# A quarter of the retention's value projection at the turn from feed-forward to mixing, and residual rows in spent W_out tiles

## The chip, the cores and the metric

The kernel runs on one core of a Trainium2 chip. The metric is the device time of one execution in microseconds (us): the median of several runs. The engines are TensorE (PE: matmuls; PEld: its weight loads), VectorE (DVE), ScalarE (ACT), GpSimd (POOL) and SyncE (SP), which here only issues DMAs. DMAs issued from POOL stand in POOL's queue, those from SP in SP's. Each engine works through its own instructions in order.

## What is computed

One layer of a bidirectional encoder trunk for 1024 tokens of width 1024, all in float32: a feed-forward layer, token mixing (retention and neighbourhood attention), and a second feed-forward layer, each between two RMS norms.

```python
def reference(x, ...):
    h = _swiglu(_rms_norm(x, ffn1_pre_norm), ffn1_w_in, ffn1_w_out)      # 1024 -> 2 x 2816 -> 1024
    x = x + 0.5 * _rms_norm(h, ffn1_post_norm)
    m = _token_mixing(_rms_norm(x, mix_pre_norm), w_mix_in, ...)
    x = x + _rms_norm(m, mix_post_norm)
    h = _swiglu(_rms_norm(x, ffn2_pre_norm), ffn2_w_in, ffn2_w_out)
    return x + 0.5 * _rms_norm(h, ffn2_post_norm)

def _token_mixing(u, w_in, ...):
    rq, rk, rv, rg, nq, nk, nv, g_ret, g_na = jnp.split(u @ w_in, points, axis=-1)
    y = _bidirectional_retention(rotary(rq), rotary(rk), rv)              # rv: 1024 tokens x 1024
    y_ret = (silu(rg) * headnorm(y)) @ w_ret_out
    y_na = _neighborhood_attention(nq, nk, nv, rel_bias) @ w_na_out       # nv: 1024 tokens x 512
    return (sigmoid(g_ret) * y_ret + sigmoid(g_na) * y_na) @ w_out
```

The change touches the end of the first feed-forward layer, the projection `rv`, and the order in which that projection is computed.

## The kernel before

**Matmuls.** Every float32 operand is split into a high part (a rounding cast on ACT, line 61) and a low part (a subtraction on DVE, line 62). A product then takes three matmuls into one PSUM bank (`mm3`, lines 88 to 90): high by high, high by low, low by high. One call of `mm3` on 128 x 512 outputs is called a unit here. Weights come by `load_w`: one DMA of 512 KB from SP into a `wraw` buffer (line 72, four buffers), then two halves (`piece`), each split into a `wh` and a `wl` buffer (eight of each). PSUM has six banks tagged `ps` and two tagged `pt`.

**The first feed-forward layer** works with a 2 x 2 block scheme (Winograd's): seven products per block. Its second half, `ffn_out`, runs 77 steps: seven products (`a11, s1, s2, s3, a22, a12, s4`) of 11 steps each. W_out is held as four blocks of three tiles each (`tiles`; `tiles[1][0]` is the block b21, last read by the product a12). Product s4, steps 66 to 76, is the last one. As its four banks finish, the function `p3` completes the token tiles 4 to 7 (512 to 1023): squares, the scale from the norm (line 98, on POOL), the residual sum (line 659, on DVE), the store of the new row to x1 (line 660, on SP), and the next layer's norm (line 670, on DVE). The residual row of a token tile, 128 x 1024 values, is fetched by `xload`, for tiles 4, 5 and 6 at steps 68, 69 and 70, and for tile 7 after the end of tile 6. Tiles 0 to 3 take spent W_out tiles for it; tiles 4 to 7 take `wraw` buffers.

**The turn.** The normalized tiles 4 to 7 then have to be transposed on PE (`flip`, line 127) and combined into the operands of the next Winograd scheme (`put`, lines 282 to 294: a22, s3, s1, s2, s4, each split into high and low). The eight tiles of s1 to s4 share eight places with the W_out blocks b21 and b22 and two result tiles. PE gets other work between the flips from `first()`: the neighbourhood value projection nv of tokens 0 to 511 (`vproj(wnv, ...)`, 32 units, whose first two weight tiles are loaded ahead at steps 65 and 66), then the leading products of the first three jobs of the mixing projections (`mx.leads()`, 24 units). `Filler` hands out units: `FLIP_FILL` says how many stand before each of the four flips (8 each) and how many between a flip and the last split of its tile (2). What is left runs at once after the last flip.

**Mixing projections.** The 14 jobs of `mx.run` compute nq, nk, rq, rk, rg and two gates; the tokens 512 to 1023 of nv follow after the fourth job.

**Attention and retention.** `na_cores` (neighbourhood attention) and then `ret_cores` (retention) have many short matmuls with chains over DVE and ACT between them. A second filler, `products()`, supplies units between them: the retention's values rv in two halves of columns, each over the token groups (0,1,2), (3,4,5), (6,7), then the remaining gates, then the output projection of the attention. In a group of `vproj` each weight tile serves two steps of k for each token tile of the group. `NA_FILL` gives 12 units at first and 2 + 2 per iteration (34 iterations); `RET_FILL` gives 14 at first and, for each of the four heads, 2, then 2 in each of 7 backward steps, 4, 2, and 3 + 0 + 1 in each of the 8 forward steps.

**Order.** The program is written in one order; a scheduler at build time gives each instruction the priority of its place in the text, gives out buffers as they come free, and fixes the order of each engine's queue. On the chip that order is kept.

Of the kernel before, what the change touches and what calls it, by code (L numbers as in the profile page):

```python
# [10 lines left out]
F32 = mybir.dt.float32  # L11
# [7 lines left out]
P = 128  # L19
# [8 lines left out]
NHP = 4  # L28

NA_FILL = (12, 2, 2)  # L30
RET_FILL = (14, 2, 2, 4, 2, 3, 0, 1, 2)
FLIP_FILL = (8, 8, 8, 8, 2)
LOADS = (6, 9, 12, 15, 18, 22, 28, 33, 38)
NA_UNITS = ((0, 0, 0), (3, 1, 0), (1, 0, 1), (1, 0, 2), (4, 1, 1), (4, 1, 2), (2, 0, 3), (5, 1, 3))
KEY_OFF = (0, 8, 24, 32)
# [638 lines left out]
def ffn_out(c, tiles, q, blocks, w_out, gl, ep, tail, side={}):  # L674
# [3 lines left out]
    nc = c.nc  # L678
# [3 lines left out]
    later, rest, flips, xs = [], [], [], {}  # L682
# [8 lines left out]

    def xload(t):

        if t < 4 or ep.pre is None:
            tile = (tiles[0][1] + tiles[0][0])[t // 2]
            xs[t] = tile[:, t % 2 * 2:t % 2 * 2 + 2].rearrange("p k f -> p (k f)")
            nc.sync.dma_start(xs[t], ep.resid(t))
        else:
            xs[t] = c.raw(ep.resid(t))


    order = []
# [31 lines left out]
    def p7(u, b):  # L734
        tt(q[3][:, u], b, q[1][:, u], ALU.add)

        def more():
            xload(u)
            add(q[1][:, u], q[1][:, u], q[2][:, u], ALU.add)
            add(q[2][:, u], q[3][:, u], q[2][:, u], ALU.add)  # L740
            ep.square(u, 1, q[2][:, u], spare[u])
        later.extend((more, None))
# [17 lines left out]
    def p3(u, b):  # L760
        e = tt(q[1][:, u], b, q[1][:, u], ALU.add)
        out = q[1][:, u] if ep.pre is not None else q[3][:, u]
        ep.square(4 + u, 1, q[1][:, u], b if ep.pre is not None else spare[2 + u % 2], out, nc.vector if u == 3 else nc.gpsimd)
        g = ep.steps(4 + u, xs[4 + u], (q[0][:, u], out))
        next(g)
        rest.append(g)
        if u > 0:
            with c.tc.issue_after(e.ins):
                next(rest[u - 1])
        if u == 3:  # L770
            next(g)
        if ep.pre is not None:
            flips.extend(next(rest[j]) for j in ((), (), (0,), (1, 2, 3))[u])
        if u == 2 and 7 not in xs:
            xload(7)
# [32 lines left out]
    for n, (i, k) in enumerate(steps):  # L808
# [11 lines left out]
        if later and i > 3:  # L820
            f = later.pop(0)
# [377 lines left out]
def trunk_layer(ctx: ExitStack, tc, x, xt, g1a, w1i, w1o, g1b, gma, wmt, wnv, wrv, logits, dtab, rope, bias,  # L1199
                wro, wno, wmo, gmb, g2a, w2i, w2o, g2b, out):  # L1200
    nc = tc.nc
# [5 lines left out]
    c = Core(tc, const, wpool, psum, dram)  # L1207
# [3 lines left out]
    def dt(name, shape):  # L1211
        return dram.tile(shape, F32, name=name)
# [3 lines left out]
    d = {  # L1216
        "a21": dt("a21", [P, 4, 512]),
        "nq": dt("nq", [NHP, P, S]), "nk": dt("nk", [NHP, P, S]), "nv": dt("nv", [16, 64, 512]), "nvg": dt("nvg", [4, 4, P, 512]),
        "no": dt("no", [NHP, P, S]), "rq": dt("rq", [RH, P, S]), "rk": dt("rk", [RH, P, S]),
        "rv": dt("rv", [TT, P, D]), "rg": dt("rg", [8, P, S]), "ry": dt("ry", [8, P, S]),  # L1220
        "sr": dt("sr", [8, P, S]), "sn": dt("sn", [8, P, S]), "z": dt("z", [8, P, S]), "m": dt("m", [8, P, S]),
    }
# [6 lines left out]
    def pool(stack, name, side="left"):  # L1229
        return stack.enter_context(tc.tile_pool(name=name, bufs=1, side=side, reuse_waits="tile"))  # L1230
# [30 lines left out]
    ep = pool(ep_stack, "ep1")  # L1261
# [4 lines left out]
    ahead = {}  # L1266
# [9 lines left out]
    def xh(t, k):  # L1276

        return a21 if (t, k) == (1, 0) else wx.op(("a11", "a12", None, "a22")[2 * t + k])

    def vproj(src, groups, done):  # L1280

        for toks in groups:
            banks = {t: c.bank() for t in toks}
            for k in range(KT):
                if k % 2 == 0:
                    w = ahead.pop(k // 2) if k // 2 in ahead else c.load_w(src[k // 2])
                for t in toks:
                    tt = slice((t % 4) * P, (t % 4 + 1) * P)
                    c.mm3(banks[t], [q[:, k % 4, tt] for q in xh(t // 4, k // 4)], w[k % 2], k == 0, k == KT - 1)
                    yield  # L1290
            for t in toks:
                done(t, banks[t])

    evpool = []

    def ev():
        return evpool[0].tile([P, S], F32, tag="ev", name="ev", bufs=3)

    def done_nv(t, b):
        e = evpool[0].tile([P, 512], F32, tag="ev", name="ev", bufs=6 if len(evpool) == 1 else 4)  # L1300
        nc.scalar.copy(e, b)
        c.store(d["nv"][2 * t:2 * t + 2].rearrange("r c d -> (r c) d"), e)

    def done_rv(j):
        def f(t, b):
            e = ev()
            nc.scalar.copy(e[:, :512], b)
            c.store(d["rv"][t][:, j * 512:(j + 1) * 512], e[:, :512])
        return f


# [5 lines left out]
    mx = Pairs(c, wx, [(wmt[j[0]], wmt[j[1]]) for j in jobs], 3)  # L1317

    def first():
        yield from vproj(wnv, ((0, 1, 2, 3),), done_nv)  # L1320
        yield from mx.leads()

    fill = Filler(first())
    evpool[:] = [wx.tmp, None]
    for f, k in zip(rest, FLIP_FILL):
        fill(k)
        f = f()
        if f is not None:
            fill(FLIP_FILL[4])
            f()  # L1330
    g_stack.close()
    ep_stack.close()
    with tc.tile_pool(name="pa", bufs=1, reuse_waits="tile") as pa:
# [12 lines left out]
        for i, (_, _, f, g, fn) in enumerate(jobs):  # L1346
# [6 lines left out]
            def done(j):  # L1353
                h = j % 2
                dst = (f, g)[j // 2][:, h * 512:(h + 1) * 512]
                while swaps:
                    swaps.pop()()
                if fn == "rotary":
                    swaps.append(rotate(c, half(), parts[j], *tabs[h], dst))
                    return  # L1360
                if fn is not None:
                    nc.scalar.activation(parts[j], parts[j], fn)
                c.store(dst, parts[j])
# [7 lines left out]
            if i == NHP - 1:  # L1371
                for _ in vproj(wnv, ((4, 5, 6, 7),), done_nv):
                    pass
                for cb in range(4):
                    nc.sync.dma_start(d["nvg"][cb].rearrange("t (r c) d -> (t r) c d", r=4),
                                      d["nv"][:, KEY_OFF[cb]:KEY_OFF[cb] + 32, :])
# [2 lines left out]
    m_stack, o_stack = ExitStack(), ExitStack()  # L1379
    mix = pool(m_stack, "mix")  # L1380
    mix.tile([P, 40], F32, name="pad")
    evpool[:] = [mix]

    def gate(i, dst, halves=(0, 1)):

        w = c.load_w(wmt[i])
        e = ev()
        for h in halves:
            hs = slice(h * 512, (h + 1) * 512)
            b = c.bank()  # L1390
            for k in range(KT):
                ks = slice((k % 4) * P, (k % 4 + 1) * P)
                c.mm3(b, [p[:, ks] for p in w[k // 4]], [q[:, k % 4] for q in xh(h, k // 4)], k == 0, k == KT - 1)
                yield
            nc.scalar.activation(e[:, hs], b, AF.Sigmoid)
        hs = slice(halves[0] * 512, halves[-1] * 512 + 512)
        c.store(dst[:, hs], e[:, hs])

    def products():
        for j in range(2):  # L1400
            yield from vproj(wrv[j], ((0, 1, 2), (3, 4, 5), (6, 7)), done_rv(j))
        yield "rv"
        for i in range(4, 8):
            yield from gate(32 + i, d["sn"][i])
        for i in range(4):
            yield from gate(24 + i, d["sr"][i])
        for i in range(4, 8):
            yield from gate(24 + i, d["sr"][i], (1,))
        x1_stack.close()
        opool = pool(o_stack, "o", "right")  # L1410
        oop = [opool.tile([P, 4, S], F32R, name=f"o{q}") for q in "hl"]
        for i in range(4, 8):
            raw = c.raw(d["no"][i - 4])
            c.split(oop[0][:, i - 4], oop[1][:, i - 4], raw)
            yield from gate(24 + i, d["sr"][i], (0,))

        for i in range(8):
            if i % 2 == 0:
                w = c.load_w(wno[i // 2])
            e = ev()  # L1420
            nc.sync.dma_start(e, d["sn"][i])
            for h in range(2):
                hs = slice(h * 512, (h + 1) * 512)
                b = c.bank()
                for k in range(4):
                    c.mm3(b, [p[:, k * P:(k + 1) * P] for p in w[i % 2]], [q[:, k, hs] for q in oop], k == 0, k == 3)
                    yield
                nc.vector.tensor_tensor(e[:, hs], b, e[:, hs], ALU.mult)
            c.store(d["z"][i], e)
# [7 lines left out]
    with tc.tile_pool(name="ret", bufs=1, reuse_waits="tile") as ret:  # L1437
        ret_cores(c, ret, mix, d, dec, fill, RET_FILL)
    y_stack = ExitStack()
# [13 lines left out]
    for i0 in (0, 3, 6):  # L1453
        tiles = range(i0, min(i0 + 3, 8))
        m, z, w, banks = {}, {}, {}, {}
# [71 lines left out]
    w = [w2.tile([P, 4, 512], F32, name=f"w{i}") for i in range(12)]  # L1527
    tiles = [[[w[n] for n in m] for m in q] for q in (((11, 10, 9), (8, 7, 6)), ((2, 1, 0), (5, 4, 3)))]
# [84 lines left out]
```

## Time and profile before

| what | us |
|---|---|
| median of 3 runs | 2270.53 |
| lowest and highest run | 2268.02, 2271.82 |
| profiled execution, its own time | 2266.95 |
| span of the profiled execution, from first to last instruction | 2265.2 |

The profile lists busy time by engine, and windows of it by stretch of the span. Times in rows of the trace are microseconds from the start of the span; mean durations marked ns are nanoseconds. In a timeline a row has the start, the duration, the engine, the line of the kernel, the operation, and the tiles (out <- in); in brackets stands the idle time of that engine before it and what ended it. A row of PE lasts longer than the distance to the next one, since matmuls overlap; the pace is the distance from start to start. "Granted clock" is the share of PE's full clock that the chip granted. In the span, the first feed-forward layer ends at about 673 us, the turn follows, the mixing projections end at about 1003, attention at about 1190, and retention at about 1432.

### The profile page before, as it was taken

Reading aid. Unit: us, or ns where it says so; the run is one execution under the profiler, and the core shown is the slowest. Engines: PE = TensorE matmul, PEld = TensorE weight load, DVE = VectorE, ACT = ScalarE, POOL = GpSimd, SP = SyncE. Lnnn points to the kernel's source line nnn. Section 1 sums busy time; section 2 is a strip of 40 time slices with the busy share of each in tenths; the row PEclk is TensorE's granted clock in tenths of the full one; section 3 lists DMA queues with packets and bytes.
Section 4 is the critical chain, followed back from the end, with each engine's and each line's share of the span. In section 5 each row is a group of like instructions: output and inputs, shape, how many; then the busy total and the mean of one; then the engine's idle time right before and its main releaser. Section 6 shows DMA issues by size and latency. Waiting matters only on the chain. (4 is left out here: it accounts for less than half of the span.)

```text
span 2265.2 us, 30039 instructions
## 1 busy us (share of the span) xinstructions
PE 2204.2 (97%) x10232; PEld 1830.1 (81%) x10232; DVE 1641.4 (72%) x2928; ACT 984.5 (43%) x2054; POOL 575.8 (25%) x747
## 2 busy tenths in 40 slices
PE   6899999999998999999999999999999999999998
PEld 5688888888786887878888888887778888888886
DVE  7898878765558757769885678544998787876444
ACT  5444434332344322248885676323644343433232
POOL 1121212168521122311101222101112121215942
PEclk9999999999999999999999999999999999999999
DMA  6354434597545554557655466764345444449765
GB/s 251 134 181 150 177 130 170 187 387 294 199 174 174 180 173 134 145 181 241 217 173 174 151 230 233 259 232 144 117 156 188 149 161 147 154 157 378 283 225 180
DMA packets 150345, 439.91 MB, mean 194 GB/s; under 512 B 19056, under 2 KB 46832, under 8 KB 148080
## 3 DMA queue, kind: packets, MB, share of 16 engines
q1 hardware_dynamic: 108912, 305.84, 39.4%
q0 software_dynamic: 41280, 132.15, 16.2%
q8 instruction: 81, 1.33, 0.2%
q14 instruction: 72, 0.59, 0.1%
HBM read 297.41 MB, written 144.70 MB: 195 GB/s over the span
## 5 line engine op out<-in xcount | busy, mean ns | idle before, releaser
L62 DVE TENSOR_TENSOR wl<-wraw,wh 128x512 fp32r<-128x512 f32 x472 | 317.1, 689 | 66.3 <-ACT wh L61 66.0
L61 ACT CAST wh<-wraw 128x512 fp32r<-128x512 f32 x476 | 274.2, 618 | 169.2 <-PE ps L89 69.2
L88 PE MATMUL ps<-wh,g 128*128 128x512 f32 x484 | 188.8, 390 | 0.0
L89 PE MATMUL ps<-wl,g 128*128 128x512 f32 x484 | 188.7, 390 | 0.0
L90 PE MATMUL ps<-wh,g 128*128 128x512 f32 x484 | 188.5, 390 | 0.0
L552 ACT ACTIVATE c<-c 128x512 f32<-128x512 f32 x88 | 55.5, 632 | 208.0 <-DVE c L517 107.6
L62 DVE TENSOR_TENSOR wl<-w,wh 128x512 fp32r<-128x512 f32 x77 | 77.9, 1031 | 86.3 <-ACT wh L61 86.1
L62 DVE TENSOR_TENSOR wl<-x,wh 128x512 fp32r<-128x512 f32 x77 | 78.4, 1035 | 78.3 <-ACT wh L61 77.1
L61 ACT CAST wh<-t 128x512 fp32r<-128x512 f32 x58 | 36.0, 621 | 195.0 <-DVE t L511 194.9
L88 PE MATMUL ps<-a11h,wh 128*128 128x512 f32 x276 | 111.5, 404 | 7.9 <-ACT wh L61 7.9
L90 PE MATMUL ps<-a11h,wl 128*128 128x512 f32 x276 | 109.7, 398 | 7.3 <-DVE wl L62 7.2
L90 PE MATMUL ps<-a12h,wl 128*128 128x512 f32 x276 | 108.7, 394 | 3.4 <-DVE wl L62 3.4
L88 PE MATMUL ps<-a12h,wh 128*128 128x512 f32 x276 | 109.7, 397 | 0.5 <-ACT wh L61 0.3
L89 PE MATMUL ps<-a11l,wh 128*128 128x512 f32 x276 | 109.8, 398 | 0.1
L90 PE MATMUL ps<-a22h,wl 128*128 128x512 f32 x280 | 109.3, 390 | 0.6 <-DVE wl L62 0.6
L88 PE MATMUL ps<-a22h,wh 128*128 128x512 f32 x280 | 109.8, 392 | 0.0
L89 PE MATMUL ps<-a22l,wh 128*128 128x512 f32 x280 | 109.2, 390 | 0.0
L89 PE MATMUL ps<-a12l,wh 128*128 128x512 f32 x276 | 108.2, 392 | 0.0
L89 PEld LDWEIGHTS ps<-wl,g 128*128 128x128 f32 x484 | 90.9, 188 | 19.1 <-DVE wl L62 0.5
L90 PEld LDWEIGHTS ps<-wh,g 128*128 128x128 f32 x484 | 90.9, 188 | 18.8
L88 PEld LDWEIGHTS ps<-wh,g 128*128 128x128 f32 x484 | 90.9, 188 | 18.7
L88 PE MATMUL ps<-s2h,wh 128*128 128x512 f32 x232 | 91.9, 396 | 6.6 <-ACT wh L61 6.5
(438 smaller groups left out, 6411.4 us busy)
## 6 DMA issues: line engine op xcount, KB each, us to landing
wraw<-in_dram SPq DMA_DIRECT2D x202, 512.0 KB, 4.5
g<-g0s SPq DMA_DIRECT2D x44, 512.0 KB, 4.2
g<-g1s SPq DMA_DIRECT2D x44, 512.0 KB, 4.9
g<-g0a SPq DMA_DIRECT2D x33, 512.0 KB, 3.3
g<-g1a SPq DMA_DIRECT2D x33, 512.0 KB, 4.5
g0s<-gth POOLq DMA_DIRECT2D x44, 256.0 KB, 4.7
g0s<-cmb POOLq DMA_DIRECT2D x44, 256.0 KB, 3.7
g1s<-gth POOLq DMA_DIRECT2D x44, 256.0 KB, 4.6
```

Source lines behind the costliest of these rows:

```text
L61: self.done = [nc.scalar.copy(h, src).ins, (eng or nc.vector).tensor_tensor(l, src, hf, ALU.subtract).ins]
L62: (eng or nc.vector).tensor_tensor(l, src, hf, ALU.subtract).ins]
L88: mm(ps, a[0], b[0], start=start, stop=False)
L89: mm(ps, a[0], b[1], start=False, stop=False)
L90: mm(ps, a[1], b[0], start=False, stop=stop)
L552: nc.scalar.activation(gate[j], gate[j], AF.Silu)
```

## The change

Two things are changed.

1. `xload` puts the residual rows of tiles 4 to 7 into the first two tiles of the spent W_out block b21 (`tiles[1][0]`), and no longer into `wraw` buffers.
2. The units of the first half of columns of rv for tokens 0 to 511 (32 units, a quarter of rv) move from `products()` to `first()`, between the nv units and the leading products. `products()` then begins with the token groups (4,5) and (6,7) for that half; the second half keeps its three groups. `FLIP_FILL` rises from 8 to 12 units before each flip, and the fill in each forward step of the retention falls from 3 to 2. `half_ev` chooses the buffer into which a value bank is evicted, by stage, and `vproj` takes weights loaded ahead only where it is told to.

```diff
-RET_FILL = (14, 2, 2, 4, 2, 3, 0, 1, 2)
-FLIP_FILL = (8, 8, 8, 8, 2)
+RET_FILL = (14, 2, 2, 4, 2, 2, 0, 1, 2)
+FLIP_FILL = (12, 12, 12, 12, 2)
...
     def xload(t):
-        if t < 4 or ep.pre is None:
-            tile = (tiles[0][1] + tiles[0][0])[t // 2]
-            xs[t] = tile[:, t % 2 * 2:t % 2 * 2 + 2].rearrange("p k f -> p (k f)")
-            nc.sync.dma_start(xs[t], ep.resid(t))
-        else:
-            xs[t] = c.raw(ep.resid(t))
+        tile = (tiles[0][1] + tiles[0][0] if t < 4 or ep.pre is None else (None, None, *tiles[1][0]))[t // 2]
+        xs[t] = tile[:, t % 2 * 2:t % 2 * 2 + 2].rearrange("p k f -> p (k f)")
+        nc.sync.dma_start(xs[t], ep.resid(t))
...
-    def vproj(src, groups, done):
+    def vproj(src, groups, done, begun=False):
...
-                    w = ahead.pop(k // 2) if k // 2 in ahead else c.load_w(src[k // 2])
+                    w = ahead.pop(k // 2) if begun and k // 2 in ahead else c.load_w(src[k // 2])
...
-    evpool = []
+    evpool, mixing = [], "mixing"
...
+    def half_ev():
+        if evpool[-1] is mixing:
+            return ev()[:, :512]
+        return evpool[0].tile([P, 512], F32, tag="ev", name="ev", bufs=6 if len(evpool) == 1 else 4)
+
     def done_rv(j):
         def f(t, b):
-            e = ev()
-            nc.scalar.copy(e[:, :512], b)
-            c.store(d["rv"][t][:, j * 512:(j + 1) * 512], e[:, :512])
+            e = half_ev()
+            nc.scalar.copy(e, b)
+            c.store(d["rv"][t][:, j * 512:(j + 1) * 512], e)
...
     def first():
-        yield from vproj(wnv, ((0, 1, 2, 3),), done_nv)
+        yield from vproj(wnv, ((0, 1, 2, 3),), done_nv, True)
+        yield from vproj(wrv[0], ((0, 1, 2, 3),), done_rv(0))
         yield from mx.leads()
...
-    evpool[:] = [mix]
+    evpool[:] = [mix, mixing]
...
     def products():
         for j in range(2):
-            yield from vproj(wrv[j], ((0, 1, 2), (3, 4, 5), (6, 7)), done_rv(j))
+            yield from vproj(wrv[j], (((4, 5), (6, 7)), ((0, 1, 2), (3, 4, 5), (6, 7)))[j], done_rv(j))
```

`done_nv` takes its buffer from `half_ev` in the same way.

More of the change, by code (lines that the diff above doesn't have):

```diff
@@ L1292, in vproj @@
                 done(t, banks[t])
-    evpool = []
+    evpool, mixing = [], "mixing"
     def ev():
         return evpool[0].tile([P, S], F32, tag="ev", name="ev", bufs=3)
+    def half_ev():
+        if evpool[-1] is mixing:
+            return ev()[:, :512]
+        return evpool[0].tile([P, 512], F32, tag="ev", name="ev", bufs=6 if len(evpool) == 1 else 4)
     def done_nv(t, b):
-        e = evpool[0].tile([P, 512], F32, tag="ev", name="ev", bufs=6 if len(evpool) == 1 else 4)
+        e = half_ev()
         nc.scalar.copy(e, b)
@@ L1305, in f @@
         def f(t, b):
-            e = ev()
-            nc.scalar.copy(e[:, :512], b)
-            c.store(d["rv"][t][:, j * 512:(j + 1) * 512], e[:, :512])
+            e = half_ev()
+            nc.scalar.copy(e, b)
+            c.store(d["rv"][t][:, j * 512:(j + 1) * 512], e)
         return f
```

## The prediction, made before the changed kernel ran

> **What bounds the kernel now.** First the page: how long, and which engine is full.
>
> ```profile
> span 2265.2 us, 30039 instructions
> PE 2204.2 (97%) x10232; PEld 1830.1 (81%) x10232; DVE 1641.4 (72%) x2928; ACT 984.5 (43%) x2054; POOL 575.8 (25%) x747
> L62 DVE TENSOR_TENSOR wl<-wraw,wh 128x512 fp32r<-128x512 f32 x472 | 317.1, 689 | 66.3 <-ACT wh L61 66.0
> L61 ACT CAST wh<-wraw 128x512 fp32r<-128x512 f32 x476 | 274.2, 618 | 169.2 <-PE ps L89 69.2
> ```
>
> TensorE (PE) has work 97% of the span, so an edit pays only where PE waits, and matmuls that are moved pay only if they land in such a wait and leave no new one behind. The last two rows price one split of a weight half, which I call a piece: 0.618 us on ACT, 0.689 us on DVE.
>
> Second, the windows of 5 us around the turn from feed-forward to mixing (columns: length; PE, PEld, DVE, ACT, POOL busy with instructions; granted clock; DMA share; GB/s), and last the turn in one window.
>
> ```profile
> 685.00:690.00 5.00, 1.41 (x9) 0.84 (x7) 3.47 (x6) 2.84 (x6) 1.33 (x2) 1.00 0.72 243
> 690.00:695.00 5.00, 4.10 (x12) 3.15 (x13) 4.44 (x9) 3.99 (x8) 0.73 (x1) 0.66 0.54 164
> 705.00:710.00 5.00, 4.36 (x20) 2.93 (x19) 5.00 (x9) 4.23 (x9) 2.92 (x5) 1.00 0.99 319
> 715.00:720.00 5.00, 2.33 (x8) 1.86 (x9) 5.00 (x10) 0.89 (x2) 0.00 (x0) 0.87 0.15 29
> 720.00:725.00 5.00, 5.00 (x19) 4.02 (x18) 5.00 (x10) 1.95 (x4) 0.56 (x1) 0.79 0.61 236
> 673.08:728.49 55.41, 46.89 (x201) 36.72 (x200) 50.20 (x85) 28.57 (x57) 9.48 (x16) 0.94 0.53 177
> ```
>
> PE is idle in holes, DVE is full, and the granted clock falls to 0.66 and 0.79 after the holes. The turn lasts from the first matmul of the neighbourhood value projection (673.08) to the first product of the projections (728.49). Third, PE's timeline, for the price of a matmul and of the holes.
>
> ```profile
> 673.08 0.39 PE L88 MATMUL ps<-wh,a11h 128*128 128x512 f32 x1
> ...
> 678.53 1.04 PE L127 MATMUL pt<-ident,q 128*128 128x128 f32 x8
> 679.33 0.48 PE L88 MATMUL ps<-wh,a11h 128*128 128x512 f32 x1
> ...
> 690.17 0.50 PE L88 MATMUL ps<-a11h,wh 128*128 128x512 f32 x1 [3.77 <-ACT wh L61]
> ...
> 692.42 0.63 PE L89 MATMUL ps<-wl,a12h 128*128 128x512 f32 x1
> 692.85 0.63 PE L90 MATMUL ps<-wh,a12l 128*128 128x512 f32 x1
> ...
> 717.67 0.50 PE L90 MATMUL ps<-a11h,wl 128*128 128x512 f32 x1 [3.35 <-DVE wl L62]
> ```
>
> From 673.08 to 678.53 PE makes 24 matmuls: 0.227 us each; eight transposes take 0.80 us. After the hole of 3.77 us one matmul takes 0.43 us. The window's 201 instructions are 168 matmuls (32 units of the value projection and 24 of the leading products, three matmuls each), 32 transposes and one at the edge. At full pace that is 168 x 0.227 + 32 x 0.10 = 41.3 us; it took 55.41. **The turn loses 14.1 us**, in holes and in the slow matmuls after them. This is the most that the edit at the turn can earn.
>
> Why the holes? SP's timeline, its waits, and DVE's.
>
> ```profile
> 638.58 15.07 SPq L625 DMA_DIRECT2D g<-g0s  x6
> 669.27 5.13 SPq L660 DMA_DIRECT2D x<-wraw  x4
> 676.91 0.33 SPq L72 DMA_DIRECT2D wraw<-in_dram  x1
> 678.12 3.85 SPq L660 DMA_DIRECT2D x<-wraw  x4
> 683.02 19.40 SPq L72 DMA_DIRECT2D wraw<-in_dram  x5
> SPq L72 <- DVE q L670: 7.8, 4, 3.6
> L670 DVE SCALAR_TENSOR_TENSOR q<-wraw,rstd,gain x8: 743/746/753, 675.4 to 687.6; 128x512 f32<-128x512 f32 x8
> 690.07 0.68 DVE L62 TENSOR_TENSOR s3l<-cmb,s3h 128x512 fp32r<-128x512 f32 x1
> 690.66 0.69 DVE L62 TENSOR_TENSOR wl<-wraw,wh 128x512 fp32r<-128x512 f32 x1
> ```
>
> The residual rows of tiles 4 to 7 sit in all four wraw buffers, and each is free only when its tile is normalized (L670). So SP issues nothing from 654 to 669, and the third weight tile of the value projection leaves at 676.91. Its halves then queue on ACT and DVE among the work for tiles 4 to 7, and the hole of 3.77 us is their wait. The second hole (3.35 us) comes because PE has nothing left but the leading products, whose pieces stand behind tile 7's Winograd sums on a full DVE.
>
> **The change, part by part.**
>
> *Residual rows.* The four loads of 512 KB stay on SP at steps 68, 69, 70 and after tile 6; only their place moves, into two spent W_out tiles. The new wait: these two are among the eight places that s1 to s4 of tiles 4 to 7 take over, so a split into them stands on ACT and DVE behind the norm of tile 7, and PE behind that. That norm's last row starts at 687.6 and ends at 688.3; the first such split on DVE is at 690.07. I cost it at nothing (at most the 3.3 us from 685, where today's holes begin, to 688.3, in rival A). What it frees: four weight tiles can load while SP is silent from 654 to 669. They cannot be split at once: the four pieces held ahead and the last four of the W_out product fill the eight wh and wl buffers until 673. So they compete with the epilogue of tiles 4 to 7 from 673 on.
>
> *More units at the turn.* 32 units of three matmuls of the retention's value projection (tokens 0 to 511, first half of columns) move here: 96 x 0.227 = 21.8 us of PE, so 41.3 + 21.8 = 63.1 us at full pace. With them come 4 weight loads on SP, ahead of those for the leading products; 8 pieces, 8 x 0.618 = 4.9 us on ACT and 8 x 0.689 = 5.5 us on DVE; 4 evictions and 4 stores on POOL's queue, behind the stores of nv:
>
> ```profile
> L1307 ACT COPY ev<-ps x16: 575/587/604, 1024.7 to 1170.9; 128x512 f32<-128x512 f32 x16
> 705.19 0.56 POOL L68 DMA_DIRECT2D nv<-ev  x1 [3.90 <-ACT ev L1301]
> 707.97 0.50 PE L88 MATMUL ps<-a12h,wh 128*128 128x512 f32 x1 [0.26 <-ACT ev L1301]
> ```
>
> ACT gains 4.9 + 2.3 = 7.2 us on 28.57, POOL 2.2 on 9.48: both fit. DVE comes to 50.20 + 5.5 = 55.7 of 63.1 us, so PE bounds the turn on the whole. The flips now stand 14 units apart (12 + 2): 14 x 0.68 + 0.8 = 10.3 us, for which DVE has 11 operations of a tile and about four pieces, 15 x 0.59 = 8.9 us (0.59 from one DVE start to the next, 690.07 to 690.66). What is late next: (a) the fourth weight tile: unit 24 comes at 673.08 + 24 x 0.68 + 0.8 = 690.2, and the places where its pieces fit are those of today's third tile, 690.66 to 691.35: 1.2 us; (b) six banks hold 4 + 4 accumulators, so two of the new ones wait for evictions: the row shows 0.26 us, I take 0.3; (c) the new evictions write to buffers that open only after the last flip: 1.0, between 0 and about 5 us (were they to wait for tile 7's sums). Left at the turn: 2.5 us. It earns 14.1 - 2.5 = **11.6 us**; between 6 and 13.
>
> A gap that is short costs no clock here:
>
> ```profile
> 870.21 0.50 PE L90 MATMUL ps<-a11h,wl 128*128 128x512 f32 x1 [2.39 <-DVE wl L62]
> 850.00:900.00 50.00, 47.61 (x210) 38.89 (x208) 34.38 (x54) 14.00 (x26) 12.58 (x19) 1.00 0.50 138
> ```
>
> After 2.39 us the clock stayed at 1.00; after 3.35 us it fell. So my 2.5 us, in pieces, carries no slow stretch.
>
> *What leaves the attention stage.* Fill there stays 12 + 34 x 4 = 148 units, but begins with token groups of two: a weight tile then serves 4 units, not 6. The first 32 units use 16 pieces where they used 10.7; by unit 128 the sum is 44 against 48.
>
> ```profile
> 1018.07 0.45 PE L909 MATMUL ps<-k,qh 128*128 128x384 f32 x1 [3.21 <-ACT qh L64]
> 1010.00:1020.00 10.00, 6.79 (x29) 5.33 (x28) 7.07 (x21) 4.67 (x10) 0.00 (x0) 0.95 1.03 292
> 1020.00:1030.00 10.00, 8.80 (x38) 6.86 (x38) 8.99 (x35) 7.72 (x23) 1.08 (x2) 0.87 0.47 162
> 1050.00:1060.00 10.00, 10.00 (x61) 8.91 (x61) 9.97 (x29) 8.73 (x25) 1.41 (x1) 1.00 0.71 232
> ```
>
> Eight pieces are ready when the stage begins and DVE has room until 1020, which hides most; the fourth row shows PE full with DVE at 9.97 of 10. Not hidden at worst: 5.3 x 0.689 = 3.7 us, and two casts ahead of qh, 1.2 us. At best two banks held instead of three win back 1 us. I take a loss of **1.0 us** (-1 to 4.9), nearest to the fourth row.
>
> *What leaves the retention.* Its fill falls from 14 + 4 x 54 to 14 + 4 x 46 units: each of 32 forward steps loses one, 0.68 us. The total (384, now 352) still just covers both stages.
>
> ```profile
> 1236.38 0.22 PE L88 MATMUL ps<-qh,kh 128*128 128x128 f32 x1
> 1241.12 0.22 PE L88 MATMUL ps<-qh,kh 128*128 128x128 f32 x1
> 1400.00:1410.00 10.00, 10.00 (x66) 8.99 (x64) 8.59 (x24) 5.81 (x17) 2.85 (x5) 1.00 0.63 226
> ```
>
> A step takes 4.74 us and PE does not wait; it becomes 4.06. In the last head DVE works 0.859 x 4.74 = 4.07 us per step, of which the lost unit takes some along, so it about fills the new step. Not shown by any row: whether the chains still fit. Bounds: 0, and 21.8 us if no step gets shorter. I take **1.0**, nearest to the row at 1050, where a full DVE leaves PE busy.
>
> One rule speaks against early splits.
>
> ```profile
> L62 DVE TENSOR_TENSOR wl<-w,wh 128x512 fp32r<-128x512 f32 x77 | 77.9, 1031 | 86.3 <-ACT wh L61 86.1
> 669.37 1.68 POOL L649 TENSOR_TENSOR q<-q,gain 128x512 f32<-128x512 f32 x1 [0.92 <-ACT ps L648]
> ```
>
> Splits in the W_out products, where POOL subtracts, take 1.031 us against 0.689, and POOL multiplies in the epilogue too. The Trainium skill (SBUF — State Buffer, Who interferes with whom) says that a DVE instruction with two SBUF inputs and a GpSimd instruction that reads SBUF block one another; the rows agree. By it two early pieces cost 0.7 us more of DVE; the sum is without it, since DVE has 7.4 us to spare.
>
> **Sum:** -14.1 + 2.5 + 1.0 + 1.0 = -9.6 us. The profiled execution took 2266.95 us (span 2265.2), so 2257.3 like for like; the median of the runs is 3.6 us above it, so I forecast a median of 2270.5 - 9.6 = **2260.9 us**.
>
> **The rivals.**
>
> A: the turn stays bound by DVE. For it: DVE is at 5.00 of 5 in the windows from 705 on, and 5.5 us are added. Against: PE gets 21.8 us. Priced as 7 us left in place of 2.5 (half of today's loss): -5.1, **2265.4 us**. That the edit doesn't do what it says belongs here: weights land early, but nobody splits them before the old time.
>
> B: the start of attention gives it back. For it: PE waits there already, and the clock falls to 0.87. The 4.9 us above, and one more slow stretch of 3.1 us (the five windows quoted from the turn lack 7.8 us of busy time; the other 14.1 - 7.8 = 6.3 us are mostly slow matmuls after two holes, half of it for one): 8.0 in place of 1.0, so -2.6, **2267.9 us**: no change that can be measured. The Trainium skill (TensorE: Matmul & The Clock Gate, Part 1) lets the clock fall only after an idle window of about 3.4 us; by that rule B's slow stretch needs a hole of that length and without one B gives 2270.5 - 9.6 + 3.9 = 2264.8. Here the clock was at 0.87 after a hole of 3.21 us, so the trace decides for the dearer price.
>
> C, on the other side: the retention lived on its fill. With a unit less, the state's chain on DVE and ACT ends after PE in each step, and every step keeps its 4.74 us: 20.8 us worse than the sum, +11.2, **2281.7 us**. It decides from (9.6 + 1.0)/32 = 0.33 us of wait per step (no gain) and 0.47 us (slower). Against: PE is at 10.00 of 10 in the row above and does not wait.
>
> **How the numbers follow.** A measurement of this kernel tells about 0.2% (4.5 us) from no change. Forecast 0.52 (all faster); A 0.20 (0.16 faster, 0.04 same); B 0.15 (0.04 faster, 0.11 same); C 0.13 (0.02 same, 0.11 slower). Faster 0.72, same 0.17, slower 0.11. Range: the turn at 13 and no losses elsewhere gives about 2257; I set 2256 for the unknown banks, and 2269 above takes in A, B and 1.4 us of spread. C is left out.
>
> **What would show it.** After: SP loads weights before 669; the turn, now with about 297 PE instructions, takes 64 to 67 us with no hole over 2 us and the clock at 1.00; its loads of rv weights precede the leading ones. A start of attention with 1018's wait under 4.5 us; forward steps of 4.0 to 4.2 us with PE at 10.00. Wrong if PE waits for wl again near 690 or 717 (A), for qh or wh near the start of attention (B), or for sf, a or a bank in the forward steps (C).

## The result and the profile after

| | before | after |
|---|---|---|
| median of 11 runs each, us | 2269.62 | 2265.35 |
| lowest and highest run | 2265.7, 2273.15 | 2262.83, 2266.69 |
| ratio after to before, 95% interval | | 0.9979 (0.9971 to 0.9987) |
| span of the profiled execution | 2265.2 | 2261.0 |

The changed kernel is faster by 0.21%, some 4 to 5 us; forecast were 9.6 us and 2260.9. The sign is right, the size about half. The page of the kernel after, its span and engines and the price of a split:

```profile
span 2261.0 us, 30078 instructions
PE 2203.0 (97%) x10232; PEld 1828.8 (81%) x10232; DVE 1637.7 (72%) x2928; ACT 993.5 (44%) x2062; POOL 576.7 (26%) x747
L62 DVE TENSOR_TENSOR wl<-wraw,wh 128x512 fp32r<-128x512 f32 x472 | 316.2, 686 | 55.0 <-ACT wh L61 54.5
```

The page hardly moves: the same 10232 matmuls, and PE still at 97%. A gain that is lost again elsewhere cannot be seen here, so the stages have to be set side by side. The windows of the turn after the change (columns as in the prediction), with its waits on PE and SP's loads:

```profile
670.53:734.63 64.10, 63.76 (x297) 52.86 (x296) 54.51 (x92) 33.86 (x68) 13.31 (x20) 1.00 0.55 185
690.00:695.00 5.00, 4.92 (x24) 4.17 (x25) 5.00 (x9) 2.90 (x6) 0.72 (x1) 1.00 0.75 252
715.00:720.00 5.00, 5.00 (x24) 4.14 (x23) 5.00 (x10) 3.25 (x7) 1.00 (x2) 1.00 0.79 265
```

```profile
PE pt L127 <- DVE cmb L290: 0.3, 1, 0.3
```

```profile
629.29 0.42 SPq L72 DMA_DIRECT2D wraw<-in_dram  x1
...
634.74 0.33 SPq L72 DMA_DIRECT2D wraw<-in_dram  x1
...
677.98 0.33 SPq L72 DMA_DIRECT2D wraw<-in_dram  x1
...
688.19 23.79 SPq L72 DMA_DIRECT2D wraw<-in_dram  x7
```

PE is busy through the turn, with one wait of 0.3 us and the clock at 1.00. DVE is at least as full as before (5.00 of 5 in both windows, 4.44 and 5.00 before), but PE no longer runs out of work while DVE catches up. The rows of SP at 629.29 and 634.74 bring weights; at the same places, 631.63 and 637.29, the kernel before loaded residual rows.

In the retention the two kernels differ in another way. PE's waits from the first head's first score to the end of the last head: in the kernel before the view has no row (no wait that it lists); after, it has three.

```profile
PE ps L88 <- DVE y L1117: 2.2, 5, 0.7
PE ps L89 <- DVE vl L62: 1.3, 1, 1.3
PE pt L1132 <- ACT yn L1123: 0.9, 1, 0.9
```

The forward steps did get shorter. The first score matmul of four steps of the first head, in PE's timeline of the kernel after:

```profile
1242.93 0.22 PE L88 MATMUL ps<-qh,kh 128*128 128x128 f32 x1
1246.99 0.22 PE L88 MATMUL ps<-qh,kh 128*128 128x128 f32 x1
1251.05 0.23 PE L88 MATMUL ps<-qh,kh 128*128 128x128 f32 x1
1255.55 0.23 PE L88 MATMUL ps<-qh,kh 128*128 128x128 f32 x1
```

Two of these steps take 4.06 us, the last 4.50. The table has the length of each stage, from its first matmul to the next stage's in PE's timeline (to within one matmul). A unit is 3 x 0.227 = 0.68 us; 32 units are 21.8 us. "Heads" runs from the first score of the first head to the end of the last head.

| stage, us | before | after | difference | of it units moved | lost or earned | forecast |
|---|---|---|---|---|---|---|
| turn | 55.41 | 64.10 | +8.7 | +21.8 | -13.1 | -11.6 |
| projections | 274.64 | 276.03 | +1.4 | 0 | +1.4 | 0 |
| attention, with the gap before it | 188.81 | 189.88 | +1.1 | 0 | +1.1 | +1.0 |
| to the first score | 29.30 | 29.29 | 0 | 0 | 0 | 0 |
| heads | 212.72 | 199.09 | -13.6 | -21.8 | +8.1 | +1.0 |
| sum | 760.88 | 758.39 | -2.5 | 0 | -2.5 | -9.6 |

The other 1.7 us between the two spans lie outside: the turn began 2.55 us earlier, in code that the change leaves alone, and what follows the heads took 0.9 us longer. Over the 13 profiles of this document the turn's start varies by 3.1 us and the part behind the heads by 4.6 (830.7 to 835.2), with work there that none of them changes but for the place of four loads ahead of the turn. So the stages explain where time went; what the change is worth in all is better read from the ratio. Below, the *loss* of a stage is its length less its matmuls at full pace (0.2267 us for 512 columns, 0.12 for 256, 0.10 for 128 or a transpose). The loss of the four heads was 4.5 us before and 12.7 after.

### The profile page after: what moved, and what is told of

The parts are those of the page before. It is cut to its first block, busy times and chain, and to the rows that moved or that the text cites. A ratio compares the mean times of both kernels' runs of the same rounds, so it can differ in the third digit from the quotient of the medians.

```text
span 2261.0 us, 30078 instructions
## 1 busy us (share of the span) xinstructions
PE 2203.0 (97%) x10232; PEld 1828.8 (81%) x10232; DVE 1637.7 (72%) x2928; ACT 993.5 (44%) x2062; POOL 576.7 (26%) x747
## 4 chain that ended last, share of the span: by engine, by line
PE 79%; DVE 7%; issue 7%; POOL 2%; DMA 2%; ACT 2%; SPq 0%; POOLq 0%; DVEq 0%; ACTq 0%
PE ps L90 24%; PE ps L88 24%; PE ps L89 24%; PE pt L89 1%; PE pt L90 1%; PE pt L88 1%; POOL rstd L98 1%; PE ps L906 1%; PE pt L925 1%; DVE wl L62 1%; POOL ry L68 1%; ACT wh L61 0%; DMA vraw<-rv 0%; DMA kraw<-nk 0%; DMA g0s<-gth 0%
## 5 line engine op out<-in xcount | busy, mean ns | idle before, releaser
L90 PE MATMUL ps<-wh,g 128*128 128x512 f32 x484 | 188.3, 389 | 0.0
```

Source lines behind the costliest of these rows:

```text
L90: mm(ps, a[1], b[0], start=False, stop=stop)
```

## The experiments

What each run left: the ratio to the kernel before, measured together with it (95% interval), and the stage lengths of its profile:

| run | ratio | turn | projections | attention | to first score | heads |
|---|---|---|---|---|---|---|
| before | 1 | 55.41 | 274.64 | 188.81 | 29.30 | 212.72 |
| after | 0.9979 (0.9971 to 0.9987) | 64.10 | 276.03 | 189.88 | 29.29 | 199.09 |
| e1 | 1.0 (0.9991 to 1.0009) | 54.41 | 274.63 | 187.77 | 29.29 | 213.92 |
| e2 | 0.9986 (0.9977 to 0.9995) | 67.30 | 276.04 | 189.71 | 29.30 | 199.02 |
| e3 | 0.9988 (0.9979 to 0.9997) | 64.06 | 275.84 | 189.82 | 29.25 | 200.55 |
| e4 | 0.9999 (0.999 to 1.0008) | 64.07 | 276.07 | 189.54 | 24.59 | 205.87 |
| e5 | 0.9958 (0.9945 to 0.997) | 64.02 | 274.64 | 188.52 | 29.29 | 191.42 |
| e6 | 0.9964 (0.9951 to 0.9978) | 64.02 | 274.63 | 188.33 | 23.93 | 201.81 |
| e7 | 0.9989 (0.9979 to 0.9998) | 64.02 | 276.08 | 172.82 | 28.66 | 220.17 |
| e8 | 0.9942 (0.9929 to 0.9954) | 64.10 | 275.88 | 189.83 | 29.28 | 191.96 |
| e9 | 0.9984 (0.9973 to 0.9996) | 55.27 | 274.64 | 188.04 | 29.29 | 212.68 |
| e10 | 0.9943 (0.993 to 0.9956) | 64.03 | 274.64 | 191.66 | 26.50 | 191.27 |
| e11 | 0.9969 (0.9958 to 0.9981) | 64.09 | 276.05 | 188.12 | 29.30 | 198.94 |

### Which half of the change fills the turn (e1, e2)

e1 is the kernel before with the residual rows of tiles 4 to 7 in spent W_out tiles, and nothing else. e2 is the changed kernel with these rows back in `wraw`.

```diff
 e1, to the kernel before (e2, to the kernel after: the reverse)
-            xs[t] = c.raw(ep.resid(t))
+        tile = (tiles[0][1] + tiles[0][0] if t < 4 or ep.pre is None else (None, None, *tiles[1][0]))[t // 2]
```

> The kernel before, with only the residual rows moved into the spent W_out tiles. Theory (each edit removes one hole of the turn): the third and fourth weight tiles are split before PE asks for them, the hole of 3.8 us near 690 and its slow matmuls go, the hole before the leading products stays; the turn loses 6 to 8 us instead of 14.1, retention as before (4.5 us lost in the four heads); 6 to 8 us faster than before. Rival (the extra units alone did it): the turn still loses 12 to 14 us and the time is that of before within 2 us.

> The changed kernel with the residual rows of tiles 4 to 7 back in wraw buffers. Theory: the first hole of the turn returns (near 690, about 4 us and the slow matmuls after it), the second stays away; the turn loses 5 to 8 us instead of 1.05, retention gives back about 8 as in the changed kernel; 0 to 3 us slower than before. Rival (the units alone did it): the turn loses under 2.5 us, and the time is that of the changed kernel, 4 to 5 us faster than before.

e1 gained nothing, against its theory; its turn lost 13.1 us, as the rival had it, and shows why. PE's timeline of e1, the two rows with holes of over 2 us, and the windows behind them:

```profile
691.54 1.11 PE L127 MATMUL pt<-ident,q 128*128 128x128 f32 x4 [3.43 <-ACT cmb L279]
...
715.84 0.80 PE L90 MATMUL ps<-a11h,wl 128*128 128x512 f32 x1 [4.45 <-DVE wl L62]
```

```profile
690.00:695.00 5.00, 3.46 (x11) 2.94 (x12) 4.79 (x9) 3.62 (x7) 0.73 (x1) 0.66 0.45 116
...
715.00:720.00 5.00, 4.16 (x10) 3.30 (x11) 5.00 (x10) 1.19 (x2) 0.00 (x0) 0.50 0.41 111
```

The first hole is still there, 18.1 us into the turn (17.1 before) and nearly as long (3.43 for 3.77 us), but now ends with the bank that the next flip needs. ACT's rows behind that:

```profile
690.38 0.62 ACT L61 CAST s3h<-cmb 128x512 fp32r<-128x512 f32 x1 [4.35 <-DVE cmb L283]
690.91 0.58 ACT L279 COPY cmb<-pt 128x512 f32<-128x512 f32 x1
```

The copy that empties the bank stands on ACT behind a cast that waits 4.35 us for a Winograd sum on DVE. So the weights were the last to arrive in the kernel before, not the only late ones: beside them stood the flips' own chain over DVE. With the weights in time PE used up its units sooner and then waited for the flip. The turn got 1.0 us shorter.

e2 has the units without the freed buffers: one wait of 1.84 us for a wl, a turn of 67.30, so 9.9 us of the 13.1. The rows are thus worth 3.2 us beside the units and 1.0 us alone. The turn lost 4.2 us, less than the theory's 5 to 8 and more than the rival's 2.5, and the time was not 0 to 3 us slower than before but 0.14% faster. The units fill the turn; the buffers only finish it. In the ratio e2 and the changed kernel can't be told apart.

### Where the retention lost 8 us: first guesses (e3, e4)

The waits for y at L1117 end with a bank, so e3 gives the scores banks tagged `pt` and leaves all six `ps` banks to the rest. e4 takes the units from the backward steps (one less in each of 7 per head) and leaves the forward steps at 3.

```diff
 e3
-        sc = c.bank()[:, :P]
+        sc = c.bank("pt", 2)[:, :P]
 e4
-RET_FILL = (14, 2, 2, 4, 2, 2, 0, 1, 2)
+RET_FILL = (14, 2, 1, 4, 2, 3, 0, 1, 2)
```

> The changed kernel with the retention's score products in the two banks tagged pt, so that one of six ps banks less is asked for in each forward step; nothing else differs. Theory (the shorter steps wait for a PSUM bank that the y of the step before releases late): PE's waits for y in the four heads (2.2 us) go and the heads lose 8 to 10 us instead of 12.7; 6 to 9 us faster than before. Rival (DVE and ACT have no room for steps of 4.06 us, whatever the banks): the heads lose 12 to 13 us still, the waits move to other tiles, and the time is that of the changed kernel.

> The changed kernel with 3 units again in each forward step of the retention and 1 instead of 2 in each backward step (28 units less in all where the changed kernel has 32 less). Theory (it is the forward step, with its chain over ACT, POOL and DVE, that cannot be shortened): forward steps take 4.74 us as before, the heads lose 5 to 8 us instead of 12.7, 8 to 12 us faster than before. Rival (any unit taken from the retention costs, since its DVE work needs the time): the heads lose 12 us or more, and the time is that of the changed kernel or worse.

e3 moved the wait and didn't shorten it. In the first head the seventh step (from one first score matmul to the next) fell from 4.50 to 4.07 us, and the crossing (from the eighth of these matmuls to the first of the next head) grew from 26.90 to 27.74; the four heads lost 14.1 us. A shortage of banks is where the wait shows, not what makes it long. e4 was no faster than the kernel before. Its first head's backward steps, inside "to the first score", gave up their seven units free of charge (29.30 to 24.59, 7 x 0.68 = 4.8), but those of the later heads, which follow a forward pass, did not: the heads lost 14.7 us and not the theory's 5 to 8, although all forward steps but one of 6.38 us and two of 4.9 to 5.0 took no longer than 4.77 again. PE waited there above all for splits on DVE (`vl`: 3.2 us in three waits of the backward steps). The rival, that a unit taken from the retention costs wherever it stood, holds for e4, apart from the first head.

### The loop through ACT (e5, e8, e9)

ACT's and DVE's timelines of the kernel after, in the second head:

```profile
1307.01 0.42 ACT L1120 ACTIVATE yn<-y 128x256 f32<-128x256 f32 x1 [0.73 <-DVE y L1118]
1307.33 0.19 ACT L1120 ACTIVATION_READ_ACCUMULATOR yn<-y 128x1 f32 x1
1307.42 0.28 ACT L61 CAST ah<-a 128x128 fp32r<-128x128 f32 x1
1308.52 0.51 ACT L1123 ACTIVATE yn<-y,rstd 128x256 f32<-128x256 f32 x1 [0.81 <-POOL rstd L98]
1308.93 0.39 ACT L61 CAST sfh<-st 128x256 fp32r<-128x256 f32 x1
1309.23 0.40 ACT L61 CAST vh<-vraw 128x256 fp32r<-128x256 f32 x1
1309.54 0.47 ACT L1115 ACTIVATE y<-ps,decq 128x256 f32<-128x256 f32 x1
```

```profile
1302.05 0.42 DVE L1118 TENSOR_TENSOR y<-ps,y 128x256 f32<-128x256 f32 x1
...
1306.55 0.42 DVE L1118 TENSOR_TENSOR y<-ps,y 128x256 f32<-128x256 f32 x1
...
1310.46 0.48 DVE L1117 SCALAR_TENSOR_TENSOR y<-ps,decq,y 128x256 f32<-128x256 f32 x1
1310.97 0.42 DVE L1118 TENSOR_TENSOR y<-ps,y 128x256 f32<-128x256 f32 x1
...
1315.49 0.42 DVE L1118 TENSOR_TENSOR y<-ps,y 128x256 f32<-128x256 f32 x1
```

Follow one turn of it. The row y is complete on DVE (1306.55); ACT squares it (1307.01), DVE and POOL make rstd of the sum, and ACT scales y by it (1308.52), after standing idle 0.81 us. Only behind that, in ACT's fixed order, come the cast of sf and the *next* step's first y (1309.54), then DVE's two operations on it (1310.46, 1310.97). Nothing in the data ties the next y to this rstd; the queue does. From one L1118 to the next it is 4.50, 4.42 and 4.52 us, and PE's step is 4.06 now. The rows fall behind by about 0.4 us per step, the banks and the two rows that may wait for their store (`left`) take that up, and in the seventh step PE stands.

The loop is no constant: over the four heads its middle turns take 4.0 to 5.5 us after the change; what makes the single turns differ was not followed up. Nor was it shorter than PE's step of 4.74 us everywhere before. The same DVE rows in the second head of the kernel before, where the line is L1121:

```profile
1299.07 0.42 DVE L1121 TENSOR_TENSOR y<-ps,y 128x256 f32<-128x256 f32 x1
1304.25 0.42 DVE L1121 TENSOR_TENSOR y<-ps,y 128x256 f32<-128x256 f32 x1
1309.23 0.42 DVE L1121 TENSOR_TENSOR y<-ps,y 128x256 f32<-128x256 f32 x1
```

They stand 5.18 and 4.98 us apart. In that head the row y starts 1.05 us after its product on PE in the first step and 4.47 us after it in the seventh, and PE never waits. So the rows already fell behind; the head ended before PE met the lag. A view of the kernel before shows the wait that was hidden, ACT's from the first score to the end of the heads:

```profile
ACT yn L1126 <- POOL rstd L98: 23.1, 31, 1.5
```

e5 moves the scaling to POOL, right behind rstd. e8 does that too, and gives ACT a copy of y of the same size, whose result is not used, so that its work is as before. e9 is the kernel before with e5's line.

```diff
 e5 (e9: the same in the kernel before)
-        nc.scalar.activation(yn, y, AF.Copy, scale=r[:, 0:1])
+        nc.gpsimd.tensor_scalar(yn, y, r[:, 0:1], None, ALU.mult)
 e8, added to that
+        yj = pool.tile([P, 256], F32, tag="yj", name="yj", bufs=1)
+        nc.scalar.activation(yj, y, AF.Copy, scale=dec.qd[:, 0, h:h + 1])
```

> The changed kernel with one operation of the retention moved: the scaling of a normalized row (yn from y and rstd, 128x256) is done on POOL right behind the rstd, not on ACT. In the changed kernel ACT stands idle 22.3 us in 29 waits for POOL's rstd, and behind each wait are queued sf's cast and the first y of the next step, on which PE's bank waits. Theory (the loop y, square, rstd, yn, next y through ACT's order takes 4.4 us and is longer than the new step of 4.06): the waits of PE for y at L1117 (2.1 us idle) go, the seventh step falls from 4.4-4.5 to 4.06, and the four heads together get shorter by 2.5 to 5 us against the changed kernel's 199.1; time 0.996 to 0.9975 of the kernel before. Rival (DVE and ACT simply have too much work at the end of a head): the last step or the crossing behind it stays as long, heads shorter by under 1 us, ratio that of the changed kernel (0.998).

> The kernel with yn scaled on POOL, and with ACT given back the work it lost: a copy of y of the same size and form (128x256 with a scale by row, about 0.51 us, 32 times), whose result nobody reads and which waits for nothing on POOL. Theory (the wait for rstd in ACT's order made the loop too long, not ACT's work): the four heads stay at 191 to 193 us, as with yn on POOL alone (191.4), against 199.1 in the changed kernel; ratio 0.995 to 0.9965. Rival (16 us of work less on ACT was what helped): the heads are back at 196 to 199 us, ratio 0.9975 to 0.9985.

> The kernel before, with yn scaled on POOL and nothing else. Theory (with a step of 4.74 us the loop of 4.4 us was hidden behind PE's fill): the heads stay at 212.7 us within 1, ratio 0.999 to 1.0005. Rival (the move is a gain of its own, whatever the fill): 4 to 8 us shorter, ratio 0.9965 to 0.998.

e5 made the heads 7.7 us shorter than in the changed kernel (199.09 to 191.42), more than the 2.5 to 5 expected; their loss is 5.0 us. PE's waits in the heads of e5 are one row:

```profile
PE pt L1132 <- POOL yn L1123: 0.8, 1, 0.8
```

The scaling itself is slower there. The group of it in e5, and in the kernel after:

```profile
L1123 POOL TENSOR_SCALAR yn<-y,rstd x32: 928/938/1458, 1237.2 to 1418.2; 128x256 f32<-128x256 f32 x32
```

```profile
L1123 ACT ACTIVATE yn<-y,rstd x32: 500/510/529, 1236.8 to 1426.0; 128x256 f32<-128x256 f32 x32
```

e8 separates the two readings of e5: with the work back on ACT and no wait for rstd there, the heads take 191.96 us. It was the wait in the queue, not ACT's load. Its ratio of 0.9942 is below the 0.995 to 0.9965 expected, and nothing in the heads accounts for that. e9 leaves the heads of the kernel before at 212.68 against 212.72: there the loop cost PE nothing. Its ratio of 0.9984, a little outside its expectation, has no counterpart in the heads and stays unexplained; the ratios of e5 and e8 may contain as much. The lengths of the heads don't depend on that: 7.7 of the 8.1 us (7.1 by e8) are the loop, shown from both sides. With this line the change brings about what was forecast for it (0.42%, 9.5 us in e5), and e5 and e8 beat both kernels.

### Where the cover stood (e6, e7)

e6 moves eight units within the retention to the last two forward steps of each head. e7 takes the units from attention instead.

```diff
 e6
-RET_FILL = (14, 2, 2, 4, 2, 2, 0, 1, 2)
+RET_FILL = (13, 2, 2, 4, 2, 2, 0, 1, 2)
-            fill(n[2])
+            fill(n[2] if h else 1)
-            fill(n[5])
+            fill(n[5] + (cc >= NC - 2))
 e7
-NA_FILL = (12, 2, 2)
-RET_FILL = (14, 2, 2, 4, 2, 2, 0, 1, 2)
+NA_FILL = (12, 2, 1)
+RET_FILL = (14, 2, 2, 4, 2, 3, 0, 1, 2)
```

> The changed kernel with eight units of the retention's fill moved: two more for each head, one in each of its last two forward steps; taken from the backward steps of the first head (seven, where the run with less backward fill lost nothing) and one from the fifteen before it. No unit is added. Theory (the end of a head lacks cover, the rest of it does not): the loss of the four heads falls from 12.7 us to 7 to 9, the time to 0.995 to 0.9965 of the kernel before. Rival (each unit taken from the retention costs 0.25 us wherever it stood): the moved units give back 2 us and cost 2, ratio 0.998.

> The changed kernel, but the units that it no longer has are taken from attention (2 + 1 per iteration for 2 + 2, 34 units) and the retention's forward steps keep 3 as before. Theory (each stage has its own slack, and the retention's middle steps had some): the heads are back at a loss of 4.5 us, attention, whose ACT works 145.6 and DVE 152.6 of 174 us, loses at least 8 us more than the 1.1 it lost already; ratio 0.998 to 1.001. Rival (attention had the slack that the retention lacks): attention becomes shorter by the whole 23 us that 34 units take, ratio 0.995.

In e6 three heads come down to losses of 1.1, 1.8 and 1.6 us (2.8, 4.0 and 2.6 after the change), and the units taken cost nothing. The third head lost 5.5 us (3.3 after the change), 2.6 of them at a new place, its second step; ACT's and PE's timelines of e6:

```profile
1329.03 0.62 ACT L61 CAST wh<-wraw 128x512 fp32r<-128x512 f32 x1 [3.95 <-DMA wraw<-in_dram]
...
1332.63 1.66 ACT L61 CAST wh<-wraw 128x512 fp32r<-128x512 f32 x3
1335.04 0.30 ACT L61 CAST ah<-a 128x128 fp32r<-128x128 f32 x1 [0.76 <-DVE a L1105]
```

```profile
1335.39 0.39 PE L88 MATMUL ps<-vh,ah 128*128 128x256 f32 x1 [1.61 <-ACT ah L61]
```

ACT waited 3.95 us for a weight's transfer, the splits of weights then stood in a bunch ahead of ah, and PE waited for ah. The sum of the four losses, 10.0 us, is above the 7 to 9 expected; the time is as expected. e7 confirms the ratio of its theory, not its split: attention lost 5.4 us more than in the changed kernel rather than 8, and the heads came back to a loss of 10.6, not 4.5, with 6.6 of it in the third head. The first two heads, with three units per step, lost 1.0 us each, as in the kernel before.

### The start of attention (e10, e11)

```diff
 e10, with e5's line
-NA_FILL = (12, 2, 2)
-RET_FILL = (14, 2, 2, 4, 2, 2, 0, 1, 2)
+NA_FILL = (16, 2, 2)
+RET_FILL = (10, 2, 2, 4, 2, 2, 0, 1, 2)
 e11, in products(); the list of groups goes with j
-        for j in range(2):
+        for j in (1, 0):
```

> The changed kernel with yn on POOL, and with four units of fill moved from the fill before the first head (14 to 10) to the start of attention (12 to 16). There PE waits 2.8 us for qh, whose loads and splits are not ready. Theory (a hole of 2.5 us at the start takes up four units of 0.68 us): the start gets shorter by 2 to 2.7 us like for like and the fourteen had slack; ratio 0.9945 to 0.995. Rival (the pieces for four more units stand on ACT ahead of qh, so the wait moves along): the same as with yn on POOL alone, 0.9958, or worse.

> The changed kernel with the two halves of columns of the retention's values in the other order: the fill of attention then begins with groups of three tokens as in the kernel before, and the groups of two come last. Theory (the 1.1 us that attention lost is the price of groups of two at its start, 16 pieces where there were 10.7): the loss of attention with its gap falls from 15.0 to about 14 us, too little for the ratio to tell (0.997 to 0.998). Rival (that loss has nothing to do with the groups): it stays at 15.

e10 is a miss. Attention takes 191.66 us, that is 188.94 without the four units (2.72 us), against 188.52 in e5: the wait for qh fell from 2.8 to 2.2 us, and another, for s, rose from 1.2 to 1.8. The four units taken from the fill before the first head cost nothing there (29.29 to 26.50). Its ratio, next to the theory's 0.9945, is that of e8, measured together with it, so it says nothing for the theory. e11 has attention 1.8 us shorter than the changed kernel, where its theory had 1. PE's waits in it come to 5.8 us against 6.3 in the changed kernel, so most of the 1.8 us is not a wait; the next section has what goes with it. And single profiles don't settle 1 us: e2, e3, e4, e5 and e6, whose code in attention is that of the changed kernel, lie between 188.3 and 189.8. The price of the groups of two stays open.

## Why the forecast was off, step by step

**The turn** came out as forecast, a little better: 64.10 us (64 to 67 expected), 297 PE instructions, clock 1.00, SP's weights before 669. The 2.5 us that I left for the fourth weight tile, the banks and the buffers were 1.0 of loss, with 0.34 of idle time. My reason for the holes was too narrow: I read the releaser of the first hole, the third weight tile, as its cause. e1 takes it away and the hole stays, since the flips' chain over DVE ends at about the same time. It did no harm to the sum, because the units that also came are what fills such a hole, whatever ends it. The freed buffers also worked earlier than I had counted: the weights left at 629.29 and 634.74, not in SP's silent time from 654 to 669.

**Attention** lost 1.1 us in the profile against 1.0 forecast, and that closeness is luck. I had priced splits that PE would wait for. PE's waits in the stage come to 6.3 us before and 6.3 us after, and the wait for qh went from 3.21 to 2.87 us. What differs is the granted clock around that wait. Windows of 20 us, from 10 us after the stage's start, before and after:

```profile
1013.13:1033.13 20.00, 15.59 (x72) 12.42 (x71) 16.95 (x55) 15.13 (x38) 2.90 (x4) 0.91 0.73 233
1020.66:1040.66 20.00, 15.88 (x68) 12.70 (x67) 16.70 (x53) 14.92 (x36) 3.47 (x4) 0.83 0.91 286
```

The clock is 0.91 and 0.83. In the same window of e1 and e11 it is 1.00, and their attention is 1.0 and 1.8 us shorter than that of the kernels they were made from. Rivals A and B did not come true: the turn's only wait is 0.3 us, and the wait for qh, which B would have lengthened, got shorter; of B only the slower clock came, and attention lost 1.1 us where B had 8.0.

**The retention is the term that was mis-sized:** 1.0 us forecast, 8.1 measured. These 7.1 us are as large as the whole gap between -9.6 and -2.5 (the 1.5 that the turn earned beyond the forecast and the 1.4 that the projections took nearly cancel). I took 1.0 because PE was at 10.00 of 10 and DVE's work per step, 4.07 us, about fitted a step of 4.06. Both are busy times. A full PE says that the chain is hidden, not by how much, and the chain here was no engine's work but a loop of about 4.4 us that contains a wait: ACT's 23.1 us for rstd in 31 waits stood in the trace of before, 0.75 us each, in front of instructions that the next step needs. Against a loop of 4.4 us the slack would have been 4.74 - 4.4 = 0.3 us per step; by the DVE rows of the second head before, 5 us apart, there was none. The edit took 0.68.

This is rival C in kind and not in size, with the sign that I had named for it, a wait for a bank in the forward steps (2.2 us in five waits). It put the point of no gain at 0.33 us of wait per step; 8.1 / 32 = 0.25. Most steps did come to 4.06, since the lag could grow for six steps before PE met it; that is why the loss appeared in the last step and the crossing, and why the single step looked right.

**The time outside the sum.** I costed the projections at nothing. They took 1.4 us more in the profiled execution, by a lower clock behind one wait of the same length. I had read that wait as too short to cost clock; it cost some in seven of the 13 profiles. The last section has the numbers.

## What to carry to other kernels

Before taking independent work out of a loop, measure the loop that it hides: the distance from one instruction to the same instruction of the next step on the *other* engines, with their waits, and compare that with the new step; busy shares don't show it. A short wait for a slow helper costs little by itself and much by what stands behind it in the queue, so let the helper do the operation that needs its result, even where it is slower at it. What ends a hole last need not be its cause: ask what would have ended it next.

## What the runs showed of the hardware

A hole of the same length left the clock alone in some executions and not in others. In all 13 profiles PE waits 2.38 or 2.39 us once in the projections, at the same matmul. Its window in the kernel after:

```profile
876.36 0.79 PE L90 MATMUL ps<-a11h,wl 128*128 128x512 f32 x1 [2.39 <-DVE wl L62]
```

```profile
850.00:900.00 50.00, 47.61 (x203) 39.00 (x202) 39.01 (x62) 17.68 (x32) 16.69 (x24) 0.97 0.59 154
```

The granted clock is 0.97 here and was 1.00 in the same window before. The slow stretch stands right behind the hole: in the first 2 us after it (876 to 878) the clock is 0.58, in the next two 0.56, then 1.00. The projections take 274.6 us in six profiles (before, e1, e5, e6, e9, e10) and 275.8 to 276.1 in the other seven. With the changed turn both kinds occur (three and seven), so the 1.4 us are a matter of the clock, not of work or waits; without the added units only the first kind was seen, in three profiles (before, e1, e9), and whether the change makes the second likelier stays open. In the same way the first 75 us, whose code is the same in all these kernels, differ between the kernel before and the kernel after in the granted clock:

```profile
0.00:75.00 75.00, 56.12 (x218) 43.14 (x218) 57.60 (x92) 42.79 (x81) 8.35 (x13) 0.95 0.51 189
```

```profile
0.00:75.00 75.00, 55.55 (x225) 42.12 (x226) 59.89 (x96) 43.70 (x83) 8.35 (x13) 1.00 0.54 190
```

It was 0.95 in the one and 1.00 in the other. Here too the slow stretches follow holes: in the kernel before the clock is 0.83 from 35 to 45 us, with a hole of 1.77 us in it, and 0.83 from 65 to 75, with one of 1.82; after the change it is 1.00 in both, with holes of 1.77 and 1.92. The turn began between 670.53 and 673.64 in the 13 profiles, with the changed code as with the code before. At the other end, the hole of 4.45 us in e1 took the window behind it down to 0.50.
